# A conv FFN with its up product in seven block products and its down product as a stage of its own

## The chip, the cores and the metric

The kernel runs on one core of a Trainium2 chip. The metric is the device time of one execution in microseconds (us), as the median of three runs. The engines have names in the rows: PE is TensorE's products, PEld its weight loads, DVE is VectorE, ACT ScalarE, POOL GpSimd, SP the engine whose queue issues most DMAs.

## What is computed

One layer of an encoder over 2048 positions of width 1024: a mixer, a cross-attention into 256 memory tokens, and a gated FFN with a depthwise convolution of width 3 over the positions, each with an RMS norm before it and a residual add, and a final norm. The change is in the FFN (D_FF is 2816, so w_up has 5632 columns):

```python
def _conv_ffn(h, w_up, b_up, conv_w, conv_b, w_down, b_down):
    S = h.shape[1]
    u = h @ w_up + b_up
    up = jnp.pad(u, ((0, 0), (1, 1), (0, 0)))
    u = conv_w[0] * up[:, :S] + conv_w[1] * up[:, 1:S + 1] + conv_w[2] * up[:, 2:] + conv_b
    gate, val = jnp.split(u, 2, axis=-1)
    return (jax.nn.silu(gate) * val) @ w_down + b_down

        h = _rmsnorm(x, norm_ffn_g[l])
        x = x + _conv_ffn(h, ffn_w_up[l], ...)
    return _rmsnorm(x, final_norm_g)
```

## The kernel before

All arrays are float32. Activations are kept transposed: 128 channels on the partitions, positions along the free axis; D = 1024 is 8 K tiles (KD), D_FF is 22 F tiles (NF). Each operand of a product is split into a high and a low part of 12 significant bits (type F32R), and mm3 (line 111) adds three products of one pass each into PSUM: high by high, high by low, low by high. A weight tile is split by split_w (line 90): the high part by GpSimd (line 96), the low part by VectorE as a subtraction (line 100).

The order in the code: mix_in, mixer, xattn (the cross-attention, which writes x2 to DRAM in column chunks), ffn (line 119). A planner orders the instructions of each engine and places the waits when the program is made. It may put an instruction ahead of others of its engine that come earlier in the code; a tile waits for the last reader of the tiles that had its place before. Pools of tiles are stacked from two sides of the same memory, and a closed pool's place is used again.

In ffn the sequence is cut in two halves of u (H = 1024), and the F tiles run in the outer loop (line 301 and on).

- prep_cols (line 167) makes h for 512 positions: the x2 columns are loaded, GpSimd multiplies by 1/rms (line 178), ScalarE rounds to the high part (line 179), VectorE makes the low part (line 180).
- up_tile (line 184) makes one of 44 F tiles of u for a half: w_up[f] is loaded and split, then two column tiles of 512 take 8 K tiles by 3 passes each (line 202) into the PSUM tile pu; ScalarE takes pu to u with the bias (line 203); VectorE makes the three taps of the convolution in three instructions for each of two column tiles (lines 210 to 213). Three columns are carried from the first half to the second (lines 192 and 206, GpSimd).
- act_tile (line 217) makes a gate tile and a value tile, silu on ScalarE, the product on VectorE (line 226), and its high and low parts (lines 227, 228), which stay in SBUF.
- down (line 231) multiplies two F tiles at a time with w_down into the PSUM tile pd, and VectorE adds each result into the accumulator acc in SBUF (line 238), which load_acc filled with x2 and the bias. The column tiles are 512 and 510 in the first half and 342 in the second; the last F tiles go by 512, 258 and 256.
- final (line 248) is the last norm, with sums of squares on ScalarE and VectorE or GpSimd, a product with ones, and 1/rms spread over the partitions by products with diagonal matrices (line 88). The first half's norm lies in the second half's loop; the last column tile's norm ends the program.

The order of a half, cut:

```python
            for g in range(0, NF, 2):
                acts = [act_tile(half, g, hts)]
                if pend and not end:
                    down(acc, *pend, by_row[half])
                acts.append(act_tile(half, g + 1, hts, ...))
                wds = [load_w(wdp, "wd", w_down[g * P:(g + 1) * P]), ...]
```

In xattn the products of probabilities and values (tile po, line 1173) come last; their weights vm lie on the right side of the memory until the last of them.

## Time and profile before

| | us |
|---|---|
| median of 3 runs | 2714.61 |
| lowest and highest | 2714.24, 2720.58 |
| span of the profiled execution | 2716.2 |
| PE busy in it | 2624.5 (97%) |
| DVE, ACT, POOL busy | 1774.6, 697.9, 703.7 |

The span runs from the first to the last instruction of one execution. Busy time of PE counts overlapping products once. In a row of a timeline the first number is the start, the second the duration; several like instructions in a row are merged (x2), and a bracket gives the idle time before the row and what ended it.

### The profile page before, as it was taken

How to read it: one execution, taken by the hardware profiler on the slowest of the kernel's cores; microseconds unless marked ns; L12 is line 12 of the kernel's file. 1: busy time of each engine (PE TensorE's matmuls, PEld its weight loads, DVE VectorE, ACT ScalarE, POOL GpSimd, SP SyncE). 2: the span in 40 equal slices, each digit the busy share in tenths (PEclk: the TensorE clock that was granted, in tenths of full speed). 3: DMA queues.
4: the chain of work that ended last, by engine and by line, in shares of the span. 5: the costliest groups of instructions: out<-in, count | busy, mean ns of one | idle time of the engine just before them, and what ended most of it. 6: DMA issues, size and time to landing. Idle time of an engine off the chain costs nothing.

```text
span 2716.2 us, 35205 instructions
## 1 busy us (share of the span) xinstructions
PE 2624.5 (97%) x13412; PEld 2267.2 (83%) x13412; DVE 1774.6 (65%) x3235; ACT 697.9 (26%) x1317; POOL 703.7 (26%) x765
## 2 busy tenths in 40 slices
PE   8999998899999999989999999999999999999998
PEld 6988996777787899988888888888778888888887
DVE  7676758778646867676555555555776775666555
ACT  4222114465312333233111111111233111111113
POOL 5232325744103332252111111112440111111112
PEclk9999998898999999999999999999999999999999
DMA  6333536655663222243111111111214111111111
GB/s 205 112 115 116 159 117 192 192 177 160 209 208 99 71 80 65 63 124 136 54 47 47 47 47 47 47 47 59 82 62 148 54 64 47 47 47 47 47 32 63
DMA packets 166001, 256.77 MB, mean 95 GB/s; under 512 B 32860, under 2 KB 101576, under 8 KB 165832
## 3 DMA queue, kind: packets, MB, share of 16 engines
q1 hardware_dynamic: 108284, 206.07, 24.3%
q10 hardware_dynamic: 57548, 48.46, 5.5%
q8 instruction: 105, 1.72, 0.3%
q14 instruction: 64, 0.52, 0.1%
HBM read 200.92 MB, written 54.73 MB: 94 GB/s over the span
## 4 chain that ended last, share of the span: by engine, by line
PE 80%; DVE 11%; DMA 3%; issue 2%; POOL 2%; ACT 1%; SPq 0%; POOLq 0%; ACTq 0%; DVEq 0%
PE pu L116 11%; PE pu L115 11%; PE pu L114 11%; PE pd L114 6%; PE pd L115 6%; PE pd L116 6%; PE pz L114 3%; PE pz L115 3%; PE pz L116 3%; PE pt L115 2%; PE pt L114 2%; PE pt L116 2%; PE po L114 2%; PE po L116 2%; PE po L115 2%
## 5 line engine op out<-in xcount | busy, mean ns | idle before, releaser
L115 PE MATMUL pu<-htl,wuh 128*128 128x512 f32 x1408 | 551.5, 392 | 4.6 <-DVE htl L180 4.6
L114 PE MATMUL pu<-hth,wuh 128*128 128x512 f32 x1408 | 549.7, 391 | 0.7 <-POOL wuh L96 0.7
L116 PE MATMUL pu<-hth,wul 128*128 128x512 f32 x1408 | 550.1, 391 | 0.0
L238 DVE TENSOR_TENSOR acc<-acc,pd 128x342 f32<-128x342 f32 (+4 forms) x416 | 239.8, 583 | 311.0 <-PE pd L116 302.3
L115 PEld LDWEIGHTS pu<-htl,wuh 128*128 128x128 f32 x1408 | 265.0, 188 | 59.9 <-DVE htl L180 6.3
L114 PEld LDWEIGHTS pu<-hth,wuh 128*128 128x128 f32 x1408 | 265.1, 188 | 53.5 <-POOL wuh L96 1.0
L116 PEld LDWEIGHTS pu<-hth,wul 128*128 128x128 f32 x1408 | 265.0, 188 | 52.8
L114 PE MATMUL pd<-ah,wdh 128*128 128x342 f32 (+4 forms) x856 | 299.8, 351 | 2.4 <-DVE acc L238 2.4
L115 PE MATMUL pd<-al,wdh 128*128 128x342 f32 (+4 forms) x856 | 300.4, 351 | 0.2 <-DVE al L228 0.2
L116 PE MATMUL pd<-ah,wdl 128*128 128x342 f32 (+4 forms) x856 | 300.2, 351 | 0.0
L203 ACT ACTIVATE u<-pu,vec 128x512 f32<-128x512 f32 x176 | 121.3, 690 | 651.0 <-PE pu L116 640.8
L96 POOL TENSOR_SCALAR wuh<-st 128x1024 fp32r<-128x1024 f32 x88 | 98.5, 1119 | 671.3 <-PE pu L115 625.8
L213 DVE SCALAR_TENSOR_TENSOR t<-u,vec,t 128x512 f32<-128x512 f32 (+2 forms) x176 | 139.1, 793 | 98.8 <-ACT u L203 96.4
L114 PEld LDWEIGHTS pd<-ah,wdh 128*128 128x128 f32 x856 | 161.5, 189 | 24.1 <-DVE acc L238 3.3
L115 PEld LDWEIGHTS pd<-al,wdh 128*128 128x128 f32 x856 | 161.9, 189 | 22.6 <-DVE al L228 0.6
L116 PEld LDWEIGHTS pd<-ah,wdl 128*128 128x128 f32 x856 | 161.7, 189 | 16.3
L210 DVE TENSOR_SCALAR t<-u,vec 128x512 f32<-128x512 f32 (+2 forms) x176 | 103.2, 589 | 90.0 <-ACT u L203 86.1
L212 DVE SCALAR_TENSOR_TENSOR t<-u,vec,t 128x512 f32<-128x512 f32 (+2 forms) x176 | 135.7, 775 | 2.2
L227 ACT ACTIVATE ah<-t 128x512 fp32r<-128x512 f32 x88 | 55.4, 633 | 262.8 <-DVE t L226 190.6
L100 DVE TENSOR_TENSOR wul<-st,wuh 128x1024 fp32r<-128x1024 f32 x88 | 112.3, 1276 | 5.6 <-POOL wuh L96 5.6
L109 DVE STREAM_TRANSPOSE pt<-p 32x256 f32<-32x256 f32 x256 | 111.5, 436 | 6.8 <-POOL p L1143 3.5
L116 PE MATMUL pz<-hth,wtl 128*128 128x512 f32 x256 | 100.9, 394 | 4.7 <-DVE wtl L100 4.7
(691 smaller groups left out, 5541.8 us busy)
## 6 DMA issues: line engine op xcount, KB each, us to landing
st<-in_w_up_dram SPq DMA_DIRECT2D x88, 512.0 KB, 3.4
st<-in_w_down_dram SPq DMA_DIRECT2D x44, 512.0 KB, 3.5
st<-in_w_t_dram SPq DMA_DIRECT2D x32, 512.0 KB, 3.9
xt<-in_x_t_dram SPq DMA_DIRECT2D x56, 256.0 KB, 3.9
zt<-zt ACTq DMA_DIRECT2D x32, 256.0 KB, 3.4
st<-in_w_kv_dram SPq DMA_DIRECT2D x16, 512.0 KB, 5.4
x_d<-xt ACTq DMA_DIRECT2D x32, 256.0 KB, 2.6
x<-x_d SPq DMA_DIRECT2D x16, 512.0 KB, 4.0
```

What stands on the lines that cost most here:

```text
L96: nc.gpsimd.tensor_scalar(hi, src, 1.0, 1.0, op0=ALU.mult, op1=ALU.mult)
L100: self.split = eng.tensor_tensor(lo, src, hi.bitcast(F32), op=ALU.subtract)
L109: self.nc.vector.transpose(out[(rb, *pre, ra)], src[(ra, *pre, rb)])
L114: mm(out, a[0], b[0], start=start, stop=False)
L115: mm(out, a[0], b[1], start=False, stop=False)
L116: mm(out, a[1], b[0], start=False, stop=stop)
L203: nc.scalar.activation(u[:, pos:pos + N], pu, AF.Identity, bias=vec[:, 0, f:f + 1])
L210: nc.vector.tensor_scalar(t, u[:, b + 1:b + n + 1], vec[:, 2, f:f + 1], vec[:, 4, f:f + 1], op0=ALU.mult, op1=ALU.add)
L212: nc.vector.scalar_tensor_tensor(t, u[:, b:b + n], vec[:, 1, f:f + 1], t, op0=ALU.mult, op1=ALU.add)
L213: nc.vector.scalar_tensor_tensor(t, u[:, b + 2:b + n + 2], vec[:, 3, f:f + 1], t, op0=ALU.mult, op1=ALU.add)
L227: nc.scalar.activation(ah[:, sl], gt[i], AF.Copy)
L238: nc.vector.tensor_tensor(acc[:, d, sl], acc[:, d, sl], pd[:, :n], op=ALU.add)
```

## The change

The up product takes a pair of F tiles, (a, b), as a matrix of two by two blocks: two F tiles by two groups of four K tiles, against two groups of K tiles by two column tiles of 512. It makes the two by two blocks of u by seven products of blocks and sums (Strassen's in Winograd's form) in place of eight. prep builds, for each of four K groups, seven operands: B11, B21, B22 and the sums T1 to T4 (B12 only enters the sums), each in high and low parts, with sums on VectorE and GpSimd. weights makes the sums of the weight blocks on GpSimd. block runs the products: x, y and z are PSUM tiles; p1, p5, u2 and u3 are partial results taken out of PSUM by ScalarE and VectorE; a further product is then added into the same bank (again). The last product of a block, with w[4], is issued after the first product of the next block (pend). The convolution's middle tap moves from VectorE to ScalarE, and each tile is one instruction of about 1022 columns in place of two of 512.

The gated product is no longer split at once: it is written to a DRAM tile act. down is a stage of its own, by chunks of 512 positions: four PSUM tiles take all 22 F tiles each, for two groups of four output tiles; act and w_down are loaded in pieces of 128 x 512 and split in passing; VectorE adds bias and x2 when a tile leaves PSUM. The accumulator acc and its adds are gone. The stages are: prep and up of the first half, prep of the second, down of the first chunk, up of the second half, down of the other three chunks. The scratch for descriptors is cut to 1024 bytes. Everything ahead of ffn is as it was, but for comments. The removed lines are the functions described above.

```diff
+    T4, T1, T2, T3, B21, B22, B11, B12 = range(8)
...
+        def prep(half, pl):
+            hs = []
+            for kk in range(4):
+                x = pl.tile([P, 4, N], F32, name="hx", tag="hx")
+                bt = pl.tile([P, 8, N], F32, name="hb", tag="hb")
...
+                    o = bt[:, (B11 if i == 0 else B21):][:, :2].rearrange("p a n -> p (a n)")
+                    nc.vector.scalar_tensor_tensor(o, xi, gk[:, 0, k:k + 1], cx.rb, op0=ALU.mult, op1=ALU.mult)
+                hi = (h3 if kk == 3 else hp).tile([P, 7, N], F32R, name="hth", tag=f"h{kk}h")
+                lo = (h3 if kk == 3 else hp).tile([P, 7, N], F32R, name="htl", tag=f"h{kk}l")
+                def split(a, b):
+                    nc.scalar.activation(hi[:, a:b], bt[:, a:b], AF.Copy)
+                    nc.vector.tensor_tensor(lo[:, a:b], bt[:, a:b], hi[:, a:b].bitcast(F32), op=ALU.subtract)
+                nc.vector.tensor_tensor(bt[:, T1], bt[:, B12], bt[:, B11], op=ALU.subtract)
+                nc.gpsimd.tensor_tensor(bt[:, T3], bt[:, B22], bt[:, B12], op=ALU.subtract)
+                nc.vector.tensor_tensor(bt[:, T2], bt[:, B22], bt[:, T1], op=ALU.subtract)
+                split(B21, B12)
+                nc.gpsimd.tensor_tensor(bt[:, T4], bt[:, B21], bt[:, T2], op=ALU.subtract)
+                split(T1, B21)
+                split(T4, T1)
+                hs.append((hi, lo))
+            return hs
...
+            def weights(fa):
+                a = raw.tile([P, 2, N], F32, name="wa", tag="raw")
+                nc.sync.dma_start(a.rearrange("p a n -> p (a n)"), w_up[fa])
+                b = raw.tile([P, 2, N], F32, name="wb", tag="raw")
+                nc.sync.dma_start(b.rearrange("p a n -> p (a n)"), w_up[fa + 1])
+                s = raw.tile([P, 2, N], F32, name="ws", tag="raw")
+                t = raw.tile([P, 2, N], F32, name="wt", tag="raw")
+                tt = nc.gpsimd.tensor_tensor
+                tt(s[:, 0], b[:, 0], b[:, 1], op=ALU.add)
+                tt(s[:, 1], s[:, 0], a[:, 0], op=ALU.subtract)
+                tt(t[:, 0], a[:, 0], b[:, 0], op=ALU.subtract)
+                tt(t[:, 1], a[:, 1], s[:, 1], op=ALU.subtract)
+                w = {}
+                for src, prods, eng in ((a, (1, 2), "act"), (s, (5, 6), "act"), (t, (7, 3), "pool"), (b[:, 1:2], (4,), "pool")):
+                    m = len(prods)
+                    hl = wp.tile([P, 2, m, N], F32R, name="w", tag=f"w{m}", bufs=4 if m == 2 else 2)
+                    if eng == "act":
+                        nc.scalar.activation(hl[:, 0], src, AF.Copy)
+                    else:
+                        nc.gpsimd.tensor_scalar(hl[:, 0], src, 1.0, 1.0, op0=ALU.mult, op1=ALU.mult)
+                    nc.vector.tensor_tensor(hl[:, 1], src, hl[:, 0].bitcast(F32), op=ALU.subtract)
+                    for j, p in enumerate(prods):
+                        w[p] = (hl[:, 0, j], hl[:, 1, j])
+                return w
...
+            def product(ps, w, slot, first):
+                for kk in range(4):
+                    sl = slice(kk * P, (kk + 1) * P)
+                    cx.mm3(ps, (w[0][:, sl], w[1][:, sl]), (hs[kk][0][:, slot], hs[kk][1][:, slot]),
+                           first and kk == 0, kk == 3, not first)
...
+            def convolve(u, f):
+                if half == 0:
+                    nc.gpsimd.tensor_copy(carry[:, f], u[:, B:B + 3])
+                t = tp.tile([P, S - B], F32, name="t", tag="t")[:, :n]
+                nc.scalar.activation(t, u[:, 1:n + 1], AF.Identity, bias=vec[:, 4, f:f + 1], scale=vec[:, 2, f:f + 1])
+                nc.vector.scalar_tensor_tensor(t, u[:, 0:n], vec[:, 1, f:f + 1], t, op0=ALU.mult, op1=ALU.add)
+                nc.vector.scalar_tensor_tensor(t, u[:, 2:n + 2], vec[:, 3, f:f + 1], t, op0=ALU.mult, op1=ALU.add)
+                return t
...
+            def done(u, f):
+                t = convolve(u, f)
+                if f < NF:
+                    nc.scalar.activation(t, t, AF.Silu)
+                    gates[f] = t
                 else:
+                    g = gates.pop(f - NF)
+                    nc.vector.tensor_tensor(t, t, g, op=ALU.mult)
+                    nc.scalar.dma_start(act[f - NF, :, c0:c0 + n], t)
...
+            def block(fa, w, pend):
+                fb = fa + 1
+                ba, bb = vec[:, 0, fa:fa + 1], vec[:, 0, fb:fb + 1]
+                x = pu.tile([P, N], F32, name="px", tag="px", bufs=2)
+                product(x, w[1], B11, True)
+                p1 = tmp.tile([P, N], F32, name="p1", tag="p1", bufs=2)
+                nc.scalar.activation(p1, x, AF.Copy)
+                if pend:
+                    pend()
+                ua, oa = u_tile(fa, "ua")
+                z = pu.tile([P, N], F32, name="pz", tag="pz", bufs=2)
+                product(z, w[5], T1, True)
+                p5 = tmp.tile([P, N], F32, name="p5", tag="p5")
+                nc.scalar.activation(p5, z, AF.Copy)
+                y = pu.tile([P, N], F32, name="py", tag="py", bufs=2)
+                product(y, w[6], T2, True)
+                u2 = tmp.tile([P, N], F32, name="u2", tag="u2")
+                nc.vector.tensor_tensor(u2, y, p1, op=ALU.add)
+                product(x, w[2], B21, False)
+                nc.scalar.activation(oa[0], x, AF.Identity, bias=ba)
+                product(z, w[3], B22, False)
+                nc.vector.scalar_tensor_tensor(oa[1], z, ba, u2, op0=ALU.add, op1=ALU.add)
+                product(y, w[7], T3, False)
+                u3 = tmp.tile([P, N], F32, name="u3", tag="u3")
+                nc.vector.scalar_tensor_tensor(u3, y, bb, p1, op0=ALU.add, op1=ALU.add)
+                ub, ob = u_tile(fb, "ub")
+                nc.gpsimd.tensor_tensor(ob[1], u3, p5, op=ALU.add)
+                done(ua, fa)
+                def rest():
+                    product(y, w[4], T4, False)
+                    nc.vector.scalar_tensor_tensor(ob[0], y, bb, p1, op0=ALU.add, op1=ALU.add)
+                    done(ub, fb)
+                return rest
+            order = [f + v for f in range(0, NF, 2) for v in (0, NF)]
+            w, pend = weights(order[0]), None
+            for i, f in enumerate(order):
+                wn = weights(order[i + 1]) if i + 1 < len(order) else None
+                pend = block(f, w, pend)
+                w = wn
+            pend()
...
+        def down(chunks, pd_, pst, pool, last):
+            dw = pool("f_dw", 1, side="right")
+            xp = pool("f_dx", 2, side="right")
+            x3p = pool("f_x3", 2, side="right")
+            sm = pool("f_s", 2, side="right")
+            def operand(src, tag, hi_eng):
+                t = dw.tile([P, N], F32, name=tag + "s", tag=tag + "s", bufs=3)
+                nc.sync.dma_start(t, src)
+                hl = dw.tile([P, 2, N], F32R, name=tag, tag=tag, bufs=4)
+                if hi_eng == "act":
+                    nc.scalar.activation(hl[:, 0], t, AF.Copy)
+                else:
+                    nc.gpsimd.tensor_scalar(hl[:, 0], t, 1.0, 1.0, op0=ALU.mult, op1=ALU.mult)
+                nc.vector.tensor_tensor(hl[:, 1], t, hl[:, 0].bitcast(F32), op=ALU.subtract)
+                return hl[:, 0], hl[:, 1]
...
+            prev = None
+            for c in chunks:
+                cs = slice(c * N, (c + 1) * N)
+                tail = last and c == chunks[-1]
+                x3 = x3p.tile([P, KD, N], F32, name="x3", tag="x3")
+                sq = []
+                for s in range(2):
+                    pd = [pd_.tile([P, N], F32, name="pd", tag="pd") for _ in range(4)]
+                    for k in range(NF):
+                        a = operand(act[k, :, cs], "da", "act")
+                        w = operand(w_down[k * P:(k + 1) * P, s * N:(s + 1) * N], "dw", "pool")
+                        for i in range(4):
+                            sl = slice(i * P, (i + 1) * P)
+                            cx.mm3(pd[i], (w[0][:, sl], w[1][:, sl]), a, k == 0, k == NF - 1)
+                        if prev and s == 0 and k == 3:
+                            final(*prev, False)
+                            prev = None
+                    for i in range(4):
+                        d = 4 * s + i
+                        xt = xp.tile([P, N], F32, name="xd", tag="xd")
+                        nc.sync.dma_start(xt, x2[d * P:(d + 1) * P, cs])
+                        nc.vector.scalar_tensor_tensor(x3[:, d], pd[i], gk[:, 1, d:d + 1], xt, op0=ALU.add, op1=ALU.add)
+                        q = xp.tile([P, N], F32, name="q", tag="sq0" if d == 0 else f"q{d}" if tail and s else "sq", bufs=1 if tail and s or d == 0 else 2)
+                        nc.scalar.activation(q, x3[:, d], AF.Square)
+                        if d == 0 or tail and s:
+                            sq.append(q)
+                        else:
+                            nc.gpsimd.tensor_tensor(sq[0], sq[0], q, op=ALU.add)
+                prev = (c, x3, sq)
+            final(*prev, last)
...
+        prep_stage(0)
+        stage(first_up)
+        prep_stage(1)
+        stage(first_down)
+        stage(second_up)
+        stage(rest_down)
...
+        act_d = dr.tile([NF, P, S], F32, name="act_d")
...
-    nc = _bacc.Bacc("TRN2", target_bir_lowering=False, num_devices=1)
+    nc = _bacc.Bacc("TRN2", target_bir_lowering=False, num_devices=1, dynamic_dma_scratch_size=1024)
```

The rest of down, its final, is the same norm as before on 512 columns, with three of eight tiles by ScalarE and GpSimd in the last chunk.

## Rows read from the trace of the kernel before

**Rows 1.** The page, parts 1 and 2: engines' busy time; granted clock by slice, tenths.

```profile
PE 2624.5 (97%) x13412; PEld 2267.2 (83%) x13412; DVE 1774.6 (65%) x3235; ACT 697.9 (26%) x1317; POOL 703.7 (26%) x765
...
PEclk9999998898999999999999999999999999999999
```

**Rows 2.** The page, part 4: the chain that ended last, shares by line.

```profile
PE pu L116 11%; PE pu L115 11%; PE pu L114 11%; PE pd L114 6%; PE pd L115 6%; PE pd L116 6%; PE pz L114 3%; PE pz L115 3%; PE pz L116 3%; PE pt L115 2%; PE pt L114 2%; PE pt L116 2%; PE po L114 2%; PE po L116 2%; PE po L115 2%
```

**Rows 3.** Windows, tile pu: stretch, length, PE, PEld, ACT busy (count), clock, DMA.

```profile
1240.00:1280.00 40.00, 40.00 (x177) 33.14 (x178) 4.80 (x7) 1.00 0.50 174
...
1232.00:2704.00 1472.00, 995.43 (x4170) 779.65 (x4170) 121.19 (x176) 1.00 0.18 59
```

**Rows 4.** Timeline of PE: the first and the last of 56 products in a row.

```profile
2639.78 0.39 PE L115 MATMUL pu<-htl,wuh 128*128 128x512 f32 x1
...
2652.25 0.40 PE L116 MATMUL pu<-hth,wul 128*128 128x512 f32 x1
```

**Rows 5.** Timeline of PE: from cross-attention to FFN, and the last down product.

```profile
1231.97 0.28 PE L116 MATMUL po<-ph,vm7l 128*128 128x256 f32 x1
1232.09 0.39 PE L115 MATMUL pu<-htl,wuh 128*128 128x512 f32 x1
...
2702.77 0.28 PE L116 MATMUL pd<-ah,ht1l 128*128 128x256 f32 x1
```

**Rows 6.** Timeline of PE: five down products of 342 columns, 24 of 512 (ends).

```profile
2199.89 0.32 PE L116 MATMUL pd<-ah,wdl 128*128 128x342 f32 x1
...
2200.52 0.31 PE L114 MATMUL pd<-ah,wdh 128*128 128x342 f32 x1
...
2652.48 0.40 PE L114 MATMUL pd<-ah,wdh 128*128 128x512 f32 x1
...
2657.82 0.39 PE L116 MATMUL pd<-ah,wdl 128*128 128x512 f32 x1
```

**Rows 7.** Groups of DVE by shape, 1240 to 2690: busy us, mean ns, idle before.

```profile
L238 DVE TENSOR_TENSOR acc<-acc,pd 128x512 f32<-128x512 f32 x96 | 65.4, 685 | 41.5 <-PE pd L116 41.5
```

**Rows 8.** Windows, all engines (PE, PEld, DVE, ACT, POOL); DMA issues to landing.

```profile
675.00:815.00 140.00, 134.20 (x640) 110.86 (x639) 80.71 (x197) 33.85 (x71) 18.30 (x13) 0.99 0.67 213
...
xt<-x_d SPq DMA_DIRECT2D x32, 256.0 KB, 3.4
```

**Rows 9.** Timeline of DVE: three operations with no GpSimd operation in their way.

```profile
1209.59 1.21 DVE L100 TENSOR_TENSOR wul<-st,wuh 128x1024 fp32r<-128x1024 f32 x1
...
1232.35 0.48 DVE L1174 SCALAR_TENSOR_TENSOR xr<-po,bo,xr 128x256 f32<-128x256 f32 x1 [2.39 <-PE po L116]
...
2649.49 0.75 DVE L213 SCALAR_TENSOR_TENSOR t<-u,vec,t 128x512 f32<-128x512 f32 x1
```

**Rows 10.** Groups of ACT by shape, 1240 to 2690.

```profile
L245 ACT ACTIVATE acc<-acc,gk 128x1022 f32<-128x1022 f32 x8 | 9.2, 1148 | 2.6 <-DMA acc<-x_d 2.2
```

**Rows 11.** POOL: one product of 512 in the timeline; group of L96, 1240 to 2690.

```profile
1198.00 1.30 POOL L178 TENSOR_TENSOR xt<-xt,rb 128x512 f32<-128x512 f32 x1 [1.40 <-DMA xt<-x_d]
...
L96 POOL TENSOR_SCALAR wuh<-st 128x1024 fp32r<-128x1024 f32 x84 | 92.9, 1105 | 663.6 <-PE pu L115 625.1 <-DMA st<-in_w_up_dram 25.9 <-DVE acc L238 7.9
```

**Rows 12.** Timeline of POOL and DVE, 1940 to 1947, at the change of halves.

```profile
1940.09 3.43 POOL L178 TENSOR_TENSOR xt<-xt,rb 128x512 f32<-128x512 f32 x2
...
1940.62 1.77 DVE L226 TENSOR_TENSOR t<-t 128x510 f32<-128x510 f32 x1
...
1943.98 2.31 DVE L100 TENSOR_TENSOR wdl<-st,wdh 128x1024 fp32r<-128x1024 f32 x1
...
1946.22 1.27 DVE L238 TENSOR_TENSOR acc<-acc,pd 128x512 f32<-128x512 f32 x2
```

**Rows 13.** Windows, all engines, at the change of halves.

```profile
1920.00:1960.00 40.00, 33.59 (x135) 25.53 (x134) 36.28 (x37) 14.66 (x22) 25.28 (x18) 0.96 0.42 125
```

**Rows 14.** Timeline of PE in the cross-attention: a product after a wait.

```profile
1186.37 0.58 PE L114 MATMUL po<-ph,vm0h 128*128 128x256 f32 x1 [3.55 <-DVE xr L1174]
```

**Rows 15.** Timeline of DVE in the tail: scalings of 128x256.

```profile
2709.96 2.05 DVE L293 SCALAR_TENSOR_TENSOR acc<-acc,gk,rb 128x256 f32<-128x256 f32 x5 [1.53 <-ACT y L286]
```

More of the change, by code (lines that the diff above doesn't have):

```diff
@@ L231, in down @@
-        def down(acc, acts, wds, order):
-            for d, c0, n in order:
-                dl = slice(d * P, (d + 1) * P)
-                sl = slice(c0, c0 + n)
-                pd = psd.tile([P, 512], F32, name="pd", tag="pd")
-                for j, (a, w) in enumerate(zip(acts, wds)):
-                    cx.mm3(pd[:, :n], (w[0][:, dl], w[1][:, dl]), (a[0][:, sl], a[1][:, sl]), j == 0, j == len(acts) - 1)
-                nc.vector.tensor_tensor(acc[:, d, sl], acc[:, d, sl], pd[:, :n], op=ALU.add)
```

256 lines of the change are left out of this document (86 added, 170 removed).

## The prediction

> **What bounds the kernel now.** I read the page from the top. TensorE is busy in 2624.5 us of 2716.2, and the row of the granted clock stands at nine tenths or more in nearly every slice, so it runs at the upper of its two levels, 2.4 GHz [rows 1]. In the chain that ended last the up product (tile pu) has 33% of the span and the down product (pd) 18% [rows 2]. Next I read the stage by windows: in forty microseconds of pure up product TensorE is busy for all forty, with 177 products [rows 3], and the timeline gives the step: 55 steps from 2639.78 to 2652.25, or 0.227 us a product of 512 columns; a row's duration of 0.39 is latency and is not used [rows 4]. Other engines are shorter there. So what counts is the number of products, and the places where the next one is not ready.
>
> The FFN now: the cross-attention's last product starts at 1231.97 and the last down product ends at 2702.77 + 0.28 = 2703.05 [rows 5]. That is 1470.8 us after 1232.25, of which 4170 up products [rows 3] take 4170 x 0.227 = 947 us. To the span's end at 2716.2 a tail of 13.1 us is left.
>
> **Up product.** Before: 44 F tiles x 2 halves x 2 tiles x 8 K tiles x 3 passes = 4224 products. After: for each pair of F tiles and half 7 block products x 4 x 3 = 84 instead of 96; 22 x 2 x 84 = 3696, of the same 512 columns. At 0.227 that is 839.0 us, 119.9 less. A block takes 84 x 0.227 = 19.07 us if nothing stalls. Weight loads go from one per product to one per product; nothing changes there.
>
> **Down product.** The columns stay. 2112 products of 512 replace 1056 of about 511 and 1584 of mostly 342. A step of 342 is 0.63 / 4 = 0.158 us, one of 512 is (2657.82 - 2652.48) / 23 = 0.232 [rows 6]: 0.461 against 0.453 ns a column, a few microseconds in all. I take 2112 x 0.2305 = 487 us (480 at the up product's 0.227, 490 at 0.232). The adds into acc (416 rows of L238, VectorE) leave; they lay beside TensorE and bring nothing. New per step of 12 products (2.77 us): two loads of 256 KB (192 GB/s), one ScalarE and one GpSimd copy of 512, two VectorE subtractions of 0.69 [rows 7]. VectorE has half the time free, and an earlier stretch moved 213 GB/s at a DMA share of 0.67 with TensorE busy in 134 of 140 us, and a load of 256 KB lands in 3.4 us [rows 8]; three are staged ahead. So it is hidden. At the end of each of eight half chunks banks and operands change over: 4 us in all (0 to 16).
>
> **VectorE and GpSimd in the up stage.** This is the cost that I cannot call hidden. First VectorE per block, own times from rows without a neighbour: low parts of the weights, 3 of 1024 columns at 1.21 and one of 512 at 0.69, 4.3; four evictions out of PSUM, 0.69 + 3 x 0.75, 2.9; the convolution's two steps on 1022 columns for two F tiles, 4 x 1.28 (0.75 for 512, 0.48 for 256, so 1.04 ns a column), 5.1; the gate's multiplication, 2 x 1.21 in every second block, 1.2. Together 13.5 us of 19.07 [rows 7, 9]. ScalarE takes the first tap (1.15 for about 1022 columns), two copies, one eviction, two high parts and the silu: some 8 us, hidden [rows 10]. GpSimd: four weight sums and one output sum of 512 at 1.30, a high part of 1024 at 1.1 and one of 512 at half, the carries, some 0.7: 8.8 us [rows 11].
>
> Each engine fits alone. But at 1940 to 1947 they run one after the other: beside GpSimd's products of 512 (two in 3.43 us instead of 2.60) a VectorE multiplication of 510 columns lasts 1.77 instead of 0.69 and a subtraction of 1024 lasts 2.31 instead of 1.21; only the two evictions out of PSUM keep their time (1.27 for two) [rows 9, 11, 12]. So operations on two SBUF tiles and GpSimd's take turns; PSUM readers do not. Then a block needs 13.5 + 8.8 - 2.9 = 19.4 us on the shared path against TensorE's 19.07. I charge the difference, rounded up for burstiness to 0.45 us a block: 44 x 0.45 = 20 us (0 if the idle moments match; 146 below). The tightest wait is u3: y must be read after the product with w[7] and before the one with w[4] adds to the same bank, with one product (2.72 us) between them, and on VectorE convolution steps stand ahead of it; what queues behind it is ob on GpSimd, then the next block.
>
> The Trainium skill (GPSIMD Engine Reference, Key points) says that GpSimd shares its SBUF interfaces with VectorE and contends with VectorE instructions that have two SBUF inputs. The trace agrees: 1.77 for 0.69. Pages aside, the sum rests on the rows.
>
> **Seams.** Before, FFN products follow the cross-attention's without a gap (1231.97, then 1232.09 [rows 5]); 4224 - 4170 = 54 of them had even been slipped into its waits. At the change of halves, where columns are prepared on VectorE and GpSimd, TensorE is busy for 33.6 us of 40 and the granted clock falls to 0.96, another 1.6 us [rows 13]. Those are the nearest rows for a seam, 0 to 8 us; where a seam has more to do I go beyond them.
> - Start. The new weights' and the fourth K group's tiles lie on the side where the cross-attention's v weights are until its last product (pool order and sizes in the code). Then a load, a ScalarE copy of 1024 and a subtraction: 3.4 + 1.15 + 1.21 = 5.8 us [rows 8 to 10], the fourth group's parts, and the clock: the first product after a wait of 3.55 us has a row of 0.58 us where 256 columns have 0.28 [rows 5, 14], the lower level. 10 us (6 to 15).
> - The second half's preparation: 3584 columns of low parts, two scalings of 1024 and two differences per K group, some 8 us of VectorE, 33 in all, traced ahead of the first down stage, whose subtractions queue behind it. That stage has 122 us to hide it, but its operands are only four steps (11 us) ahead. 10 us (0 to 24); the first operands themselves 3 (0 to 8).
> - Into the second up stage: its scratch tiles lie where the chunk's x3 is until its norm has been written out, a chain like today's tail plus four GpSimd sums, some 20 us; three products can run before the first copy is wanted. 12 us (3 to 20).
> - Into the last down stage: 3 us (0 to 8).
>
> **Small things and the tail.** Norm sums and spreads of three chunks and the second half's 1/rms: about 8 us on TensorE, like today's. The tail grows from 256 to 512 columns: an eviction, a square, sixteen more short products, five of eight scalings on VectorE that took 2.05 us for 256 columns each [rows 15], output of 512 KB for 256: 13.1 becomes 18 (15 to 22).
>
> **Sum.** 1232.3 + 839.0 + 487 + 8 + 4 + 20 + 10 + 13 + 12 + 3 + 18 = 2646.3 us for an execution like the profiled one (2716.2). The median of the runs is 2714.6, 1.6 below its span, so 2645.
>
> **Rivals.**
> 1. VectorE and GpSimd bind the up stage. If the evictions find no GpSimd work beside them and every turn is paid in full, a block takes 13.5 + 8.8 = 22.3 to 22.4 us, 3.3 over: 44 x 3.3 = 146 instead of 20, 2771 us, slower. For it: the turns at 1940 [rows 12]; against: the evictions keep their time. Without up stalls the sum is 2625, so the point that decides is (2715 - 2625) / 44 = 2.0 us a block, 21.1 us. The skill's sentence above would, taken at its worst, be this case.
> 2. Seams and change-overs at their upper ends (15, 32, 20, 8, 16, 22): 2645 + 5 + 19 + 8 + 5 + 12 + 4 = 2698. For it: the change of halves stalled even with sixteen steps of L180 on VectorE, 12 us, now it is 33. Against: most lies beside 122 us of product.
> 3. All fits: no turns paid, seams at their lower ends, down at 0.227: 1232.3 + 839 + 480 + 8 + 6 + 3 + 15 - 1.6 = 2582. For it: pure up product runs with no idle time today.
>
> **How the numbers follow.** Forecast (2610 to 2685): 0.55. All nearly fits (2582 to 2610): 0.15. Upper seams, or turns at about 1.5 us a block (2685 to 2706): 0.12. Between, within 0.3% of 2714.6 (2706 to 2723): 0.04. Slower: 0.14, of which rival 1 has 0.10 and a down stage short of loads or a seam beyond its bounds 0.04. 0.3% is about what a measurement of this kernel can tell from no change. So faster 0.82, same 0.04, slower 0.14. The range 2592 to 2712 leaves out about 0.05 below and 0.15 above.
>
> **What would show it.** Right: 3696 products on px, py, pz and 2112 on pd; blocks of 19 to 20 us; in the up stage GpSimd sums beside stretched VectorE rows; idle TensorE at four seams. Wrong: blocks over 21 us with TensorE waiting for u3 or for the weights' low parts (rival 1), down steps over 2.8 us that wait for a load, or a start after 1245.

## The result and the profile after

The changed kernel takes 2675.51 us (median of 4 runs, 2673.55 to 2678.39) beside 2716.01 us (2714.24 to 2720.58) for the kernel before in the same rounds: ratio 0.9843, 95% interval 0.9828 to 0.9858. It is faster by 1.6%; the forecast was 2645 in a range of 2592 to 2712. The profiled execution has a span of 2671.6 us; the sum of the prediction, made against such a span, was 2646.3. So the direction is right and 25 us are to be explained.

The page after, parts 1, 2 and 4 (answers to [rows 1, 2]):

```profile
PE 2533.8 (95%) x12374; PEld 2141.5 (80%) x12374; DVE 1955.7 (73%) x2944; ACT 866.0 (32%) x1442; POOL 1204.0 (45%) x1097
...
PEclk9999998799999999998999999998999999999998
...
PE 72%; DVE 15%; issue 5%; DMA 4%; POOL 2%; ACT 1%; SPq 0%; ACTq 0%; POOLq 0%; DVEq 0%
```

TensorE still sets the end, with 91 us less work; VectorE has 15% of the chain, where it had 11% before. One step further down, a window in the first up stage (columns as in [rows 8]) and the timeline of PE there (answer to [rows 4]):

```profile
1440.00:1480.00 40.00, 40.00 (x174) 32.47 (x173) 35.40 (x28) 14.39 (x17) 30.18 (x24) 1.00 0.23 80
```

```profile
1442.23 0.40 PE L115 MATMUL py<-hth,w 128*128 128x512 f32 x1
...
1444.09 0.40 PE L117 MATMUL py<-hth,w 128*128 128x512 f32 x1
```

TensorE is busy for all forty microseconds, so nothing stalls, but there are 174 products where the pure up product before had 177 [rows 3]: eight steps take 1.86 us, 0.2325 each for 0.227 [rows 4], at a granted clock of 1.00. Over both up stages the steps inside the sequence have a mean of 0.2318. VectorE and GpSimd are visibly in each other's way (groups of DVE and POOL, 1300 to 1600):

```profile
L233 DVE SCALAR_TENSOR_TENSOR t<-u,vec,t 128x1022 f32<-128x1022 f32 x31 | 57.4, 1851 | 0.0
...
L272 DVE SCALAR_TENSOR_TENSOR u<-py,vec,p 128x512 f32<-128x512 f32 x16 | 11.9, 742 | 0.0
```

```profile
L197 POOL TENSOR_TENSOR wt<-wa,ws 128x512 f32<-128x512 f32 x16 | 36.4, 2277 | 0.0
```

The last convolution step lasts 1.85 us for 1.28 without GpSimd's sums (e1_classic below), the most stretched of GpSimd's sums 2.28 for 1.30 [rows 11]; an eviction out of PSUM keeps its 0.74.

The losses lie in the other places. First down stage: TensorE's waits (engine, tile, line waited for; us, times, longest), and a window of all engines:

```profile
PE pd L116 <- DVE da L307: 10.3, 9, 2.5
PE pd L115 <- DVE x L365: 1.9, 1, 1.9
```

```profile
1680.00:1820.00 140.00, 126.98 (x517) 99.40 (x515) 108.70 (x121) 42.91 (x59) 60.27 (x58) 0.95 0.63 203
```

TensorE's waits from 1680 to 1815 add up to 12.9 us, 10.3 of them for the low parts of act (da). Some 10 us more are products that run slowly behind such waits: 517 products keep TensorE busy for 127.0 us here, where 0.227 each makes 117.4, and the granted clock falls to 0.74 from 1750 to 1770 (row under e7_prep_late).

Into the second up stage (timeline of PE):

```profile
1822.27 0.39 PE L117 MATMUL pd<-da,dw 128*128 128x512 f32 x1
1829.36 1.87 PE L315 MATMUL pr<-ones,q 128*128 128x2 f32 x8 [6.70 <-POOL q L371]
1835.13 0.77 PE L87 MATMUL rb<-diag,ones 128*128 128x128 f32 x2 [3.91 <-DVE diag L86]
...
1837.67 0.77 PE L115 MATMUL px<-hth,w 128*128 128x512 f32 x1
...
1845.20 0.80 PE L117 MATMUL px<-hth,w 128*128 128x512 f32 x1 [4.62 <-DVE w L206]
```

The norm's short products stand ahead of the first px in TensorE's queue, and then eight scalings of x3 (5.35 us of DVE, L338) stand ahead of the new weights' low parts. The tail has a chain of the same kind (PE, then DVE):

```profile
2645.73 0.39 PE L117 MATMUL pd<-da,dw 128*128 128x512 f32 x1
2645.96 0.69 PE L315 MATMUL pr<-ones,q 128*128 128x2 f32 x4
2649.32 0.38 PE L315 MATMUL pr<-ones,q 128*128 128x2 f32 x2 [2.67 <-ACT q L367]
2650.60 6.97 PE L315 MATMUL pr<-ones,q 128*128 128x2 f32 x32 [0.89 <-ACT q L367]
2659.20 2.37 PE L87 MATMUL rb<-diag,ones 128*128 128x128 f32 x8 [1.64 <-DVE diag L86]
```

```profile
2647.86 1.51 DVE L365 SCALAR_TENSOR_TENSOR x<-pd,gk,xd 128x512 f32<-128x512 f32 x2 [2.31 <-DMA xd<-x_d]
```

In the whole, in the order of the prediction's sum (us). "Waits and lower clock" is what a stage's length has left when its products are taken off at their step; the right column adds up to 2671.7:

| term | predicted | in the profile after |
|---|---|---|
| last cross-attention product ends | 1232.3 | 1230.8 |
| start of the first up stage | 10 (6 to 15) | 4.8 to the first px + 7.1 of waits and lower clock = 11.9 |
| up product, 3696 x 0.227 | 839 | 839 |
| beyond it inside the up stages | 20, turns of VectorE and GpSimd | 17.7, the step: 3696 x 0.0048 |
| down product, change-overs, small products | 487 + 4 + 8 | 479.4 (2112 x 0.227) + 7 |
| second half's preparation in the first down stage | 10 (0 to 24) | 143.35 - 527 x 0.227 = 23.7 |
| its first operands | 3 (0 to 8) | 4.5 |
| into the second up stage | 12 (3 to 20) | 15.1 to the first px + 10.2 of waits and lower clock = 25.3 |
| into the last down stage | 3 (0 to 8) | 4.4 + 2.4 of lower clock = 6.8 |
| tail | 18 (15 to 22) | 25.6 |

### The profile page after: what moved, and what is told of

The parts are those of the page before. It is cut to its first block, busy times and chain, and to the rows that moved or that the text cites. A ratio compares the mean times of both kernels' runs of the same rounds, so it can differ in the third digit from the quotient of the medians.

```text
span 2671.6 us, 34733 instructions
## 1 busy us (share of the span) xinstructions
PE 2533.8 (95%) x12374; PEld 2141.5 (80%) x12374; DVE 1955.7 (73%) x2944; ACT 866.0 (32%) x1442; POOL 1204.0 (45%) x1097
## 4 chain that ended last, share of the span: by engine, by line
PE 72%; DVE 15%; issue 5%; DMA 4%; POOL 2%; ACT 1%; SPq 0%; ACTq 0%; POOLq 0%; DVEq 0%
PE pz L115 6%; PE pz L117 6%; PE pz L116 6%; PE pd L115 5%; PE pd L117 5%; PE pd L116 5%; PE py L115 4%; PE py L117 4%; PE py L116 4%; PE px L117 3%; PE px L115 3%; PE px L116 3%; PE pt L115 2%; PE pt L116 2%; PE pt L117 2%
## 5 line engine op out<-in xcount | busy, mean ns | idle before, releaser
L116 PE MATMUL pd<-da,dw 128*128 128x512 f32 x704 | 272.2, 396 | 10.4 <-DVE da L307 10.3
L115 PE MATMUL pd<-da,dw 128*128 128x512 f32 x704 | 265.1, 396 | 10.7 <-POOL dw L306 8.8
L117 PE MATMUL pd<-da,dw 128*128 128x512 f32 x704 | 268.4, 394 | 0.5 <-DVE dw L307 0.5
L306 POOL TENSOR_SCALAR dw<-dws 128x512 fp32r<-128x512 f32 x176 | 137.7, 786 | 287.1 <-PE pd L117 190.6
L307 DVE TENSOR_TENSOR dw<-dws,dw 128x512 fp32r<-128x512 f32 x176 | 132.2, 755 | 139.4 <-POOL dw L306 139.0
L115 PE MATMUL py<-hth,w 128*128 128x512 f32 x528 | 208.5, 397 | 3.1 <-DVE u L272 3.1
L116 PE MATMUL py<-htl,w 128*128 128x512 f32 x528 | 207.9, 394 | 0.0
L117 PE MATMUL py<-hth,w 128*128 128x512 f32 x528 | 206.3, 394 | 0.0
L232 DVE SCALAR_TENSOR_TENSOR t<-u,vec,t 128x1022 f32<-128x1022 f32 (+1 forms) x88 | 132.9, 1510 | 75.5 <-ACT t L231 75.3
L116 PEld LDWEIGHTS pd<-da,dw 128*128 128x128 f32 x704 | 133.7, 190 | 43.4 <-DVE da L307 16.1
L115 PEld LDWEIGHTS pd<-da,dw 128*128 128x128 f32 x704 | 134.1, 191 | 40.2 <-POOL dw L306 10.1
L233 DVE SCALAR_TENSOR_TENSOR t<-u,vec,t 128x1022 f32<-128x1022 f32 (+1 forms) x88 | 161.6, 1837 | 0.1
L117 PEld LDWEIGHTS pd<-da,dw 128*128 128x128 f32 x704 | 134.0, 191 | 29.0 <-DVE dw L307 1.2
L117 PE MATMUL px<-hth,w 128*128 128x512 f32 x352 | 140.7, 400 | 6.1 <-DVE w L206 6.1
L307 DVE TENSOR_TENSOR da<-das,da 128x512 fp32r<-128x512 f32 x176 | 133.1, 756 | 13.1 <-ACT da L304 12.6
L115 PE MATMUL px<-hth,w 128*128 128x512 f32 x352 | 141.2, 401 | 0.0
L116 PE MATMUL px<-htl,w 128*128 128x512 f32 x352 | 139.9, 398 | 0.0
L115 PE MATMUL pz<-hth,w 128*128 128x512 f32 x352 | 139.8, 397 | 0.0
L116 PE MATMUL pz<-htl,w 128*128 128x512 f32 x352 | 138.5, 394 | 0.9 <-DVE htl L167 0.9
L117 PE MATMUL pz<-hth,w 128*128 128x512 f32 x352 | 138.9, 395 | 0.0
```

The costliest lines, as they stand in the source:

```text
L115: mm(out, a[0], b[0], start=start, stop=False, skip_group_check=again)
L116: mm(out, a[0], b[1], start=False, stop=False, skip_group_check=again)
L117: mm(out, a[1], b[0], start=False, stop=stop, skip_group_check=again)
L232: nc.vector.scalar_tensor_tensor(t, u[:, 0:n], vec[:, 1, f:f + 1], t, op0=ALU.mult, op1=ALU.add)
L233: nc.vector.scalar_tensor_tensor(t, u[:, 2:n + 2], vec[:, 3, f:f + 1], t, op0=ALU.mult, op1=ALU.add)
L306: nc.gpsimd.tensor_scalar(hl[:, 0], t, 1.0, 1.0, op0=ALU.mult, op1=ALU.mult)
```

## The experiments

The theory after the result: the gain is the 528 products that leave, TensorE alone paces the up stage, and the 25 us are seams. Against it stands the prediction's own step, that VectorE and GpSimd taking turns cost some 20 us there. Where spans are compared, the stage's own length is taken, since the part ahead of the FFN varies between runs (its last product starts at 1218 to 1239). Stages that no edit touches vary too: the first down stage from 141.6 to 145.6 us, the gap before the second up stage from 14.9 to 17.1. All runs of this section but the last, e13_all, are single ones.

**e1_classic.** All eight block products (the edit in short):

```diff
-w[1]..w[7] from a, b, s = b0 + b1 - a0, t = ..., seven products
+a0*B11 + a1*B21, a0*B12 + a1*B22, b0*B11 + b1*B21, b0*B12 + b1*B22
+bt[:, T1] = max(B12, B12)   # same cost, holds B12
```

> The up product of the new kernel with all eight block products (96 products of 512 columns for a pair of F tiles and half, in place of 84), without sums of weights and with the same number of prepared columns; the staging, the activations through DRAM and the separate down product stay. Theory (TensorE's count decides, nothing else binds the up stage): 528 products more at the step of the changed kernel, 0.227 to 0.232 us, 120 to 122 us, so about 2796 us, and the step falls to 0.227 only if the operands' order or place has to do with it. Rival (VectorE and GpSimd taking turns cost some 20 us of the up stage, as I charged): the sums are gone, so 2775 us. Second rival (the new staging is itself what gained): the time stays within 20 us of the changed kernel's 2675.

Measured: 2784.31 us, 108.8 more. The two up stages last 494.6 and 491.6 us for 438.6 and 438.3, 109.3 more in all; 528 products at 0.2318 are 122.4, less 13, by which what the stages last beyond their steps falls (20.6 us to 7.5). The time lies between the theory's 2796 and the rival's 2775 and does not decide between them; the window below does. The rest of the new form, without the seven products, is slower than the kernel before by 67 us: the seven products carry the whole gain. The second rival is out. A window, 1300 to 1600, and a convolution step there (groups of DVE):

```profile
1300.00:1600.00 300.00, 300.00 (x1295) 243.36 (x1294) 132.24 (x119) 76.84 (x80) 27.16 (x67) 1.00 0.19 69
...
L226 DVE SCALAR_TENSOR_TENSOR t<-u,vec,t 128x1022 f32<-128x1022 f32 x26 | 33.4, 1284 | 0.9
```

VectorE has half the work and GpSimd an eighth of it, and the number of products is that of the changed kernel (1294 in its row below): the step of 0.232 has nothing to do with these two.

**e2_nosums.**

```diff
-s, t: four gpsimd.tensor_tensor sums
+s, t = b, a
```

> The four GpSimd sums of weights per block are left out (their places are taken by the plain weights, so the up product is not the reference's). GpSimd loses 5.2 us of its 8.8 us a block. Theory (the up stage has slack, the extra 18 us over 0.227 a product are in TensorE's own step): 2675 us, within 4 us, step still 0.232. Rival (turns of VectorE and GpSimd cost 0.45 us a block): 20 us less, 2656 us, step 0.227.

Measured: 2665.67 us, between the theory's 2675 and the rival's 2656. The window 1300 to 1600 of the changed kernel, and of this one:

```profile
1300.00:1600.00 300.00, 299.79 (x1294) 242.98 (x1293) 261.75 (x202) 110.59 (x125) 208.14 (x171) 1.00 0.23 82
```

```profile
1300.00:1600.00 300.00, 300.00 (x1295) 243.42 (x1295) 221.25 (x201) 114.69 (x124) 84.31 (x108) 1.00 0.22 79
```

Inside the stage nothing is gained, so the turns cost TensorE nothing there. They are real: 40 us less of VectorE for the same operations, 2.6 us a block. What is gained, 5.1 us in the first up stage and 3.2 us in the gap before the second, lies at the starts, where sums stand in the first weights' way.

**e3_twosums.**

```diff
-tt = nc.gpsimd.tensor_tensor
+tt = lambda o, p, q, op: [nc.gpsimd.tensor_tensor(o, p, q, op=op) for _ in range(2)]
```

> Each of the four GpSimd sums of weights is made twice, 5.2 us more GpSimd work a block. Theory (slack): by the turns the shared path would now be 19.4 + 5.2 = 24.6 us a block; if TensorE does not feel it the time stays at 2675 us, if GpSimd's own 14 us, stretched to some 19, just fit it is up to 2690. Rival (turns bind): 24.6 against 19.1 us a block, 44 times, so 2675 + 225 = 2900 us, with TensorE waiting for the low parts of the weights or for u3.

Measured: 2808.71 us, 133 more: rival 1 of the prediction, slower than the kernel before, is there once 5.2 us of GpSimd a block are added. TensorE's and GpSimd's waits, 1300 to 1700:

```profile
PE py L115 <- DVE u L272: 38.0, 10, 4.8
```

```profile
POOL ws L193 <- DMA wb<-in_w_up_dram: 38.9, 16, 3.9
```

TensorE waits where the prediction put the tightest wait, at u3, which has to be read out of y before the next product adds to it. GpSimd has no idle time but for loads of weights; that these start late because its own sums hold the buffers is argued from the code (five buffers, four tiles a block). By stage lengths a block takes 22.85 us, of which 5.2 are new: by this estimate the shared path needs about 17.65 us a block in the changed kernel, not 19.4.

**e6_halfsums.** Only two of the four are doubled:

```diff
+tt(t[:, 0], a[:, 0], b[:, 0], op=ALU.subtract)
+tt(t[:, 1], a[:, 1], s[:, 1], op=ALU.subtract)
```

> Two of the four GpSimd sums of weights per block (those of t) are made twice: 2.6 us more GpSimd work a block, half of what the doubled sums added. With all four doubled a block took 507.6 / 22 = 23.1 and 497.6 / 22 = 22.6 us, 22.85 in the mean; less the 5.2 added this leaves 17.65 us for the path that VectorE and GpSimd share in the changed kernel, against 19.5 us of TensorE. Theory (turns are real, with 1.85 us of slack a block): 17.65 + 2.6 = 20.25 us a block, 0.75 us over, 44 times: 33 us, 2708 us. Rival (the path is the 19.4 us of my sum, so it is at its limit already): 22.0 us a block, 110 us more, 2785 us. Second rival (only GpSimd's own queue overflowed when the sums were doubled): its 142.5 us of 200 become about 170, so nothing, 2675 us.

Measured: 2713.29 us; the up stages are 13.9 and 14.3 us longer, 28 of the 33 forecast (the other 9 us lie ahead of the FFN). So the estimate holds for the stage as a whole: half the addition, 2.6 us, is mostly swallowed, as 1.85 us of slack were to be used up first. It is no steady rate, as three windows show:

```profile
1300.00:1400.00 100.00, 97.46 (x412) 78.54 (x413) 87.81 (x66) 32.35 (x38) 88.91 (x65) 0.98 0.23 81
1400.00:1500.00 100.00, 98.43 (x423) 78.83 (x422) 87.54 (x66) 37.57 (x44) 92.18 (x67) 1.00 0.22 78
1500.00:1600.00 100.00, 100.00 (x431) 80.39 (x430) 87.94 (x65) 33.21 (x39) 91.66 (x66) 1.00 0.23 83
```

A block of 20.25 us would give 415 products in each 100 us; there are 412, 423 and 431, and the changed kernel has some 432. The loss comes in bursts: four waits for u from 1300 to 1690, up to 3.6 us at once.

**e4_layout.** High and low part next to each other:

```diff
-hi, lo = tile([P, 7, N]), tile([P, 7, N]);  w: tile([P, 2, m, N])
+hl = tile([P, 7, 2, N]);                    w: tile([P, m, 2, N])
```

> High and low part of each operand of the up product lie next to each other (2 KB apart, as in the down stage, in place of 14 KB for the columns and 4 KB for the weights); nothing else is changed. Theory (place of the operands sets the step of 0.232): step 0.227, 18 us less, 2657 us. Rival (order of the blocks or the neighbours on other engines sets it): no change, 2675 us within 4.

Measured: 2678.99 us, the step at each of the twelve positions in a product the same within 1 ns. That theory falls. All these distances, before and after the edit, are multiples of 2048 bytes, so the run leaves open what e10_align moves.

**e5_repeat.**

```diff
-for kk in range(4):
+for rr, kk in ((r, k) for r in range(2) for k in range(4)):
```

> Every block product of the up stage is made twice in succession into its bank, with the same operands (so the up product comes out double and is not the reference's): 7392 products in place of 3696, and half the work of all other engines per product. In the changed kernel a product of the up stage takes 0.232 us, in the pure up stretch of the kernel before and in the new down stage 0.227. Theory A (the step is long in the products that follow a change of bank or operands): the second twelve of each pair run at 0.227, and the first twelve stay at 0.232 to 0.233. Theory B (the operands of a block product, their place or their number, set it): both twelves show the same 0.232. Theory C (VectorE and GpSimd, now at half their density, stretch the step): both go to 0.227. The time is 2675 + 3696 x 0.227 to 0.233, 3514 to 3536 us, in all of them.

Measured: 3532.03 us. The first twelve products have a mean step of 0.2330, the second twelve of 0.2308; 1295 products in 1300 to 1600 again. Half the density of the neighbours' work changes nothing (C out), and a change of bank or operands explains some 2 of the 6 ns over 0.227 (A out). B is left: the operands.

**e7_prep_late.**

```diff
-prep_stage(1)                     # ahead of first_down
+next(side, None)                  # one piece of prep(1) after each step k > 3
+x3p with one buffer (room for f_prep beside it)
```

> The preparation of the second half's columns is handed out in pieces, one after each step of the first down stage from the fifth on, in place of all of it ahead of that stage; nothing else is changed. Theory (the first down stage lost 23 us because its VectorE subtractions queue behind 33 us of preparation): the stage goes from 143.4 to 121 to 126 us, 18 to 22 us less, 2655 us. Rival (the loss comes from the loads and copies of the stage's start or from the clock, not from the order on VectorE): under 6 us less, 2670 us or more. Second rival (the pieces only move the loss to the second up stage, whose first operands are then late): the first down stage shrinks, the gap behind it grows by as much, 2675 us.

Measured: 2675.45 us. The first down stage lasts 142.97 us: the theory falls, and the number is the first rival's. The timeline of DVE in the changed kernel shows why, and I should have read it first:

```profile
1740.29 1.75 DVE L167 TENSOR_TENSOR htl<-hb,hth 128x1536 fp32r<-128x1536 f32 x1
1741.96 1.77 DVE L307 TENSOR_TENSOR dw<-dws,dw 128x512 fp32r<-128x512 f32 x1
1743.65 1.09 DVE L307 TENSOR_TENSOR da<-das,da 128x512 fp32r<-128x512 f32 x1
1744.67 3.18 DVE L167 TENSOR_TENSOR htl<-hb,hth 128x1536 fp32r<-128x1536 f32 x2
```

The planner had mixed preparation (L167) and operands (L307) already. What is short is VectorE's time: it is full for 40 us on end, with subtractions at 1.77 for 0.69, and behind it the clock falls (windows of the changed kernel):

```profile
1710.00:1730.00 20.00, 17.96 (x77) 13.67 (x76) 20.00 (x20) 7.07 (x9) 11.21 (x10) 1.00 0.71 223
1730.00:1750.00 20.00, 17.24 (x73) 13.06 (x72) 20.00 (x21) 6.96 (x9) 9.56 (x8) 1.00 0.61 200
1750.00:1770.00 20.00, 13.64 (x40) 9.49 (x39) 17.24 (x18) 6.63 (x9) 7.45 (x10) 0.74 0.48 155
```

The single x3 also came to lie where the next weights go, so the first px waits 10.18 us for their high part (its row in the timeline: ACT w); the stage behind it then ran 4.9 us shorter.

**e11_act_dw.**

```diff
-w = operand(w_down[...], "dw", "pool")
+w = operand(w_down[...], "dw", "act")
```

> In the down product the high part of the weights is copied by ScalarE in place of GpSimd; nothing else is changed. In the first down stage of the changed kernel VectorE is busy in some 118 us of 140, with rows stretched beside GpSimd, and handing the preparation out one piece per step only moved where it stood. Theory (VectorE's time, stretched by GpSimd's turns, is short in that stage): 44 copies fewer on the shared path give back 10 to 18 us, the first down stage lasts 126 to 134 us in place of 143.4, 2661 us. Rival (the order alone decides: the subtractions of the operands stand behind the preparation): under 4 us, 2675 us. Second rival (ScalarE becomes late for the first operands or the prepared columns): slower than 2678 us.

Measured: 2667.11 us; the first down stage 138.3 us, 5.1 less (the rest is ahead of the FFN). VectorE's busy time there falls from 108.7 (not the expectation's 118) to 95.3 us:

```profile
1677.00:1817.00 140.00, 127.83 (x528) 101.77 (x528) 95.33 (x124) 67.77 (x104) 35.75 (x17) 0.95 0.65 208
```

GpSimd's copies had stretched VectorE, as said (its subtractions of 512 columns fall from a mean of 0.84 to 0.70 us), but the gain is half the least that was forecast: the longest wait now is 5.1 us for an eviction (DVE x), at the change of half chunks.

**e12_spread.** With e11's edit, and e7's pieces, now two to three steps:

```diff
+if (s or k > 3) and k % 3: next(side, None)
+an unused tile that keeps x3 off the next weights' place
```

> As the run before this one (weights' high part in the down product on ScalarE), and the preparation in 24 pieces, one after two of three steps of the first down stage from the fifth on; the chunk's x3 is kept at a place that the second up stage's weights do not use. Handed out one piece per step, VectorE had 2.8 us of work to a step of 2.72 us and stood full from 1700 to 1770 as before; two pieces to three steps make 2.3 us. Theory (order and VectorE's time together): the first down stage lasts 121 to 126 us, the gap behind it stays at 15 to 16 us, 2653 us. Rival (VectorE's time alone was short, and is mended by the copies): no better than that run, within 3 us.

Measured: 2670.34 us. The first px comes 4.6 us later (1240.1 for 1235.6; 7.8 us behind the cross-attention's last product, 5.1 in the changed kernel), where nothing was edited. The first down stage lasts 135.4 us, 7.9 less in all than in the changed kernel; the theory's 121 to 126 is missed. TensorE now waits 9.1 us for ScalarE's copies (dw), which came onto the same engine as the columns' high parts. The loss moves from engine to engine.

**e8_xd.**

```diff
-xt loaded in the eviction loop, bufs=2
+if k == NF - 1: load all four xt, bufs=4
-for j in range(4): for i, q in enumerate(sq): matmul(pr...)
+for q in sq: for j in range(4): matmul(pr...)
```

> The four loads of x2 that an eviction of the down product adds are issued ahead of the last step of a half chunk, into four tiles in place of two, and the products for the norm go by the square that is ready first instead of by the row block; nothing else is changed. Theory (at the end of a chunk the evictions wait for the third and fourth of these loads, and in the tail 32 short products wait for the last square): tail 25.9 to 18 to 22 us, the gap before the second up stage 15.4 to 12 to 13 us, together 6 to 10 us less, 2667 us. Rival (the loads land in time anyway and the clock, low in these stretches, sets them): under 2 us, 2675 us.

Measured: 2675.07 us, no gain in all, but both forecast places moved: the tail falls from 25.9 to 18.3 us, the gap before the second up stage from 15.4 to 13.6. Which of the two edits did how much is not shown. The end of PE in this kernel:

```profile
2654.35 0.39 PE L117 MATMUL pd<-da,dw 128*128 128x512 f32 x1
2654.58 4.07 PE L318 MATMUL pr<-ones,q 128*128 128x2 f32 x36
2660.29 2.36 PE L87 MATMUL rb<-diag,ones 128*128 128x128 f32 x8 [1.64 <-DVE diag L86]
```

The gain was eaten by the up stages, 441.9 and 441.4 us for 438.6 and 438.3, though no line of theirs was edited, and by the first down stage, 2.7 us (146.1, little above the longest unedited one). A window of the up stage, 1300 to 1600, with 1284 products for 1294:

```profile
1300.00:1600.00 300.00, 299.49 (x1284) 240.71 (x1283) 260.80 (x200) 110.39 (x124) 208.54 (x171) 1.00 0.23 81
```

The only trace of the edit in the up stages is a tile of 32 bytes for the new products, which pushed all tiles on the weights' side by 32 bytes. That gave the next theory.

**e10_align.** An unused tile of 1216 bytes ahead of the columns:

```diff
+pad = hp.tile([P, 304], F32, name="pad")
```

> An unused tile of 1216 bytes a partition is put ahead of the prepared columns, so that the columns of the first three K groups start at the same place within 2048 bytes as the weights on the other side (1408; before the pad 192); nothing else is changed. What led here: a kernel in which a tile of 32 bytes had moved the weights, but not those columns, had an up stage of 441.9 us in place of 438.6, with other steps at each place of the sequence; the pure up stretch of the kernel before (0.227) and the new down stage (0.227) have columns and weights at the same place within 2048 bytes, the new up stage (0.232) has not. Theory (the two operands' places against each other within 2048 bytes set the step): step 0.227, both up stages together 877 to 858 us, 16 to 18 us less in all, 2658 us. Rival (it is the place of each by itself, or the order): no change or a step longer, 2672 to 2685 us.

Measured: 2671.68 us, near the rival's time, but with the theory's step: it is 0.226 to 0.227 at every position of every product (timeline of PE):

```profile
1422.11 0.39 PE L116 MATMUL py<-htl,w 128*128 128x512 f32 x1
...
1423.92 0.39 PE L115 MATMUL px<-hth,w 128*128 128x512 f32 x1
```

Eight steps take 1.81 us. The step is settled, but not the time: 1307 products in 1300 to 1600, not 300 / 0.227 = 1322:

```profile
1300.00:1600.00 300.00, 296.97 (x1307) 244.67 (x1306) 263.54 (x202) 109.12 (x125) 216.48 (x172) 1.00 0.23 80
```

TensorE now waits for VectorE's u (4.5 us in the first up stage, 4.1 in the second, up to 1.5 at once). A block takes 84 x 300 / 1307 = 19.28 us where 19.07 would be free of stalls: 0.21 x 44 = 9 us. In the second up stage 3.5 us are gained. The first lasts 448.0 us for 438.6, and begins 11.9 us behind the cross-attention's last product for 5.1, as its start (timeline of PE) is dearer:

```profile
1217.61 0.28 PE L117 MATMUL po<-ph,vm7l 128*128 128x256 f32 x1
...
1229.48 0.78 PE L115 MATMUL px<-hth,w 128*128 128x512 f32 x1
...
1258.19 1.22 PE L87 MATMUL pt<-diag,ones 128*128 128x128 f32 x4 [8.54 <-DVE diag L86]
```

TensorE waits for the diagonals that spread the norm. The whole time hides this, since that last product stands at 1217.6 for 1230.5; why it is so early, and whether the pad made the start dearer, no run shows.

**e13_all.** The pad on the weights' side, e12's and e8's edits together, in five rounds:

```diff
+pad = one.tile([P, 296], F32, name="pad")
```

> Four edits together: an unused tile (1184 bytes a partition, on the weights' side) that puts weights and columns of the up product at the same place within 2048 bytes; the high part of the down product's weights on ScalarE; the preparation in 24 pieces, two to three steps of the first down stage; the four loads of x2 ahead of a half chunk's last step, with the norm's products by the square that is ready first. Theory (the gains lie at different places and add): the two up stages at 0.227 a product lose 18 us, less some 5 us in new waits for u; the first down stage 8 us; tail and the gap before the second up stage 9 us; the span goes from 2671.6 to 2641 to 2648, and the ratio to the kernel before is 0.973 to 0.975. Rival (the shorter step is given back to VectorE, as most of it seemed to be where the pad stood on the columns' side, and the rest stays): 2655 us, ratio 0.978.

Measured: 2651.28 us median (2647.27 to 2669.58), ratio to the kernel before 0.9765, interval 0.9738 to 0.9792: better than both kernels (the changed one's interval begins at 0.9828). Its profiled span is 2645.5. By stage against the changed kernel: first up stage 433.9 for 438.6, first down 136.4 for 143.4, gap 14.4 for 15.4 (within what it varies by), second up 432.7 for 438.3, tail 18.7 for 25.9; the last product ahead of the FFN 5.3 us earlier, which no edit explains, and the first px 9.0 us behind it for 5.1. The ratio lies between the theory's 0.975 and the rival's 0.978, so it does not decide; the stages do: the parts add, and the shorter step brings some 10 us of its 18, the rest being given back to waits for u (3.2 us from 1350 to 1680, 6.2 from 1860 to 2270).

## Why the prediction came out as it did

**Bound and count: right.** TensorE sets the end; 3696 and 2112 products are there. e1_classic shows that the seven products carry the gain and that the rest of the rebuilding costs.

**VectorE and GpSimd: right mechanism, wrong term.** The 20 us stood for turns in an up stage at 0.227. In the changed kernel the turns cost nothing inside the stage (e2_nosums), and the term came out at 17.7 by another cause, the longer step. The sum of 19.4 us a block was too high by some 1.75, by the estimate from e3_twosums: it let all VectorE work but PSUM readers take turns with all of GpSimd's. That idle moments match, as the prediction's lower end had it, is likely and not shown by itself. Had the step been 0.227, the charge would have been 9 us (e10_align). So the agreement of 20 and 17.7 is an accident. Rival 1 needed only 2.6 us more GpSimd work a block to cost 28 us, and 5.2 to be slower than before: its deciding point of 21.1 us a block was well placed, its starting point was not. The Trainium skill (GPSIMD Engine Reference, Key points), which names contention with VectorE instructions of two SBUF inputs, agrees with the rows: 1.85 us for 1.28 in a convolution step, 0.74 unchanged for an eviction; it gives no size for it.

**Down product: a little better than priced.** The 487 took a step of 0.2305, between the 0.227 and 0.232 of [rows 4, 6]; it is 0.227, no change-over of the last three chunks stalls, and loads of 214 GB/s (2440 to 2640) stay hidden. 12 us too many.

**Seams: the step that failed.** "I take 10" for the preparation came out at 23.7, its upper end. I counted VectorE's 33 us against 122 us of stage, but not that operands (88 x 0.69 = 61 us) and preparation, stretched by GpSimd's copies, make 109 us of VectorE in 140, full for 40 us on end: that is no cover but a second bound. Nor did I price the clock behind its waits: 12.9 of the 23.7 are waits, some 10 slow products. "12 us (3 to 20)" into the second up stage was 25.3: I priced the norm's chain, and left out that its eight scalings stand ahead of the first low parts on VectorE, and that products after it begin at the lower clock (0.43 us a step, granted clock 0.50 from 1838 to 1846: the lower of the two levels). The tail, "15 to 22", was 25.6: two loads of x2 that could only be issued when the first two evictions had freed their tiles, and 32 short products in 6.97 us; with both mended it is 18.3, within the bounds. These three are 13.7, 13.3 and 7.6 us of the 25, the smaller seams 7, and down product, up product, change-overs and the end of the cross-attention take 16 back. The sum's last step, 1.6 us off for the median, does not hold here either: the runs' median lies 3.9 us above the profiled span, so the forecast of 2645 is 30 us short of the median of 2675.5.

Left open: what remains of the first down stage (136 us for 120), where VectorE, then ScalarE, end the waits; and the start of e10_align.

## What to carry over

Price a stage that is moved beside another by adding up the engine's whole load there, stretched rows included; "122 us to hide 33" says nothing while the 122 are not free. A term that comes out at its forecast size is confirmed only when its cause is taken away and the time goes with it. Where steps of one shape differ by 2% at full clock, look at where the operands lie before looking for a busy neighbour.

## What the hardware showed unexpectedly

The step of a 512-column product depends on where columns and weights lie against each other in a partition. The places below are start addresses less whole multiples of 2048 bytes, by the compiled placement; no profile row holds them, and of them the edits show the shifts alone (32 bytes in e8_xd, 1216 in e10_align, 1184 + 32 in e13_all). Columns and weights: 1216 and 1216, 0.227 (pure up product before); 1408 and 1408, 0.227 (new down stage); 192 and 1408, 0.232 (new up stage); 192 and 1376, 0.2333 (e8_xd, whose 32 bytes did it: 1284 products in 1300 to 1600); 1408 and 1408, 0.227 (e10_align); 192 and 192, 0.227 (e13_all). The last two moved either side, so it is the difference that counts and not the place of one.

A rule for each product by itself does not come out of this. The fourth K group's columns lie, by the code (pool f_h3), on the weights' side, so neither pad moved them against the weights; yet the last three of a product's twelve steps had a mean of 0.2325 too, and have 0.227 with either pad. Whether 2048 or a smaller divisor is what matters, no run here tells, nor why the steps repeat in a fixed pattern (0.230 to 0.235 in the changed kernel, 0.226 to 0.240 in e5_repeat).
